# The opening of a one-core transformer layer: x in four whole-tile loads, whole-tile squares, half tiles scaled on GpSimd, and a shorter refinement

## The chip, the core and the metric

The kernel runs on one core of one Trainium2 chip. The metric is the device time of one execution in microseconds (us). The kernel before has a median of 902.12 us in 3 runs (900.91 to 902.39). One execution of it was also profiled; its time is 901.98 us, of which the profile's span, from the first instruction to the last, holds 900.2 us.

Five engines work side by side and meet at semaphores: TensorE (PE for the matmuls, PEld for the weight loads that overlap them), VectorE (DVE), ScalarE (ACT), GpSimd (POOL) and SyncE (SP), which here issues nearly all the loads. Each engine runs its own instructions strictly in order.

## The reference

The reference is one layer of a diffusion backbone in fp32: 512 latent tokens x of width 1024, 256 context tokens, and a conditioning vector c. Cut to what the change touches:

```
shift, scale, ... = split(silu(c) @ w_ada + b_ada, 6)
hx = (x * rsqrt(mean(x*x) + 1e-6) * norm1_g) * (1 + scale) + shift
z  = hx @ w_in            # u, vs, q, r, ga, gb, k, v, lr
... gated linear attention, spatial gating, merge, residual
... second norm, gated convolution FFN, residual, final norm
```

The same modulation, with another vector `c_ctx`, is made for the context tokens. So before the first product with `w_in` the kernel needs two things: x normalised and turned (features on the partitions), and the first 128 columns of the shift and the scale, which need the first columns of `w_ada`.

## The kernel before

**Tiling.** Tokens come in four tiles of 128 rows, features in eight blocks of 128 columns. Every large product is made from three fp32r matmuls: each operand is split into a high part and a low part, and high by high, high by low and low by high are added up in PSUM. The matmuls of these products fill nearly all of the span.

**The opening.** `tok_load` (line 142) brings x in as eight loads of 128 by 512 fp32 (256 KB) on SP's queue, two for each token tile. Four short rows (c, c_ctx, norm1_g, b_ada) come in on ACT's queue into one tile of 72 rows, which PE turns once (line 489). While x arrives, PE runs seven matmuls on constants (line 598), whose results are thrown away. `norm_tiles` (line 542) goes over the tiles: ACT squares each half (line 519, with its sum), DVE adds the two sums and makes mean plus epsilon (lines 523 and 524), ACT makes `exp(-0.5 ln v)` as a first estimate of the reciprocal root (lines 525 and 526), DVE refines it with one Newton step in three instructions (lines 531 to 533), and DVE scales both halves (lines 536 and 540); of the last tile ACT scales the second half (line 538).

`x_turns` (line 572) then turns six of the eight feature blocks of a tile on PE (line 565), each into its own PSUM bank. For tile 0 it also makes `silu(c)` on DVE and ACT (lines 497 to 501). Tiles 2 and 3 are turned together, after the first modulation sum.

**Modulation.** The columns of shift and scale are made in six groups (four of 128 columns, two of 256). `ada_load` (line 327) loads a group's part of `w_ada`; `ada_dot` (line 625, matmuls at line 634) sums it over the features with `silu(c)` as the weights, a copy takes the sums out of PSUM (line 582 for group 0), `ada_sel` (line 638) turns them into columns with two tiny matmuls (line 643) and makes the factor `am` and the addend `bm_` on DVE (lines 647 and 653). `ada_mod` (line 655) then writes a block's high part on ACT (line 664), its exact value and its low part on DVE (lines 665 and 671), and after it come the first products (line 725): q and k of head 0 and v of heads 0 and 1, block by block, while the next group's `w_ada` arrives. After the first block ACT copies turned blocks 2, 4 and 5 out of PSUM (line 570); block 1 is copied just before it.

**What sets the order.** SP's loads go out in the order of the program: x, group 0 of `w_ada`, the first rows of q, k and v weights, group 1, the next rows, and so on (lines 372 to 389); `in_order` ties them. From `STRICT` (line 561) to line 842 the instructions of PE, ACT and DVE are tied to the order of the program as well; GpSimd and SP are not named in that tie. SP's and ACT's loads share eight semaphores in rotation, and a load that takes a semaphore waits until the earlier load on it has landed.

**Buffers.** x lies in eight of the 43 `heap` tiles, and so do the squares' unused outputs. The stream of split weights uses the pool `wp`, with five buffers each for `raw`, `wh` and `wl`; four of each belong to the first v weights `fv` from the start.

Of the kernel before, what the change touches and what calls it, by code (L numbers as in the profile page):

```python
# [16 lines left out]
P = 128  # L17
# [30 lines left out]
def backbone_kernel(  # L48
# [20 lines left out]
    def nm(s):  # L69
        cnt[0] += 1  # L70
        return f"{s}_{cnt[0]}"
# [4 lines left out]
    def late(shape, dt=F32, s="l"):  # L76
        return lp.tile(shape, dt, tag="l", name=nm(s))

    def small(n, s="s"):
        return sp.tile([P, n], F32, tag=f"sm{n}", name=nm(s))  # L80

    def mm():
        return pm.tile([P, 512], F32, tag="mm", name=nm("mm"))

    def gl():
        return pg.tile([P, 512], F32, tag="gl", name=nm("gl"))
# [48 lines left out]
    adma = nc.scalar.dma_start  # L135
    A.preload_act_table_set("natural_log_exp_and_others")

    rows_a = late([72, P], s="rows")
    for o, ap in ((0, c[0]), (8, c_ctx), (16, norm1_g[0]), (24, b_ada[0])):
        adma(rows_a[o:o + ap.shape[0] // P, :], r8(ap))  # L140

    def tok_load(ap, n, pool):
        tiles = []
        for t in range(n):
            pair = [pool([P, 512], s="xin") for _ in range(2)]
            for hf in range(2):
                dma(pair[hf], ap[t * P:(t + 1) * P, hf * 512:(hf + 1) * 512])
            tiles.append(pair)
        return tiles

    START = len(traced())
    xin = tok_load(x[0], 4, heap)

    specs = []

# [329 lines left out]
        V.tensor_copy(cols_, ps[:, :n])  # L485
        return cols_

    rows_ps = mm()
    T.transpose(rows_ps[:, :72], rows_a, ident[:72, :72])
    vec_a = const([P, 72], "vec_a")  # L490
    cT, n1g, bada = vec_a[:, 0:16], vec_a[:, 16:24], vec_a[:, 24:72]
    cs = const([P, KT, 32], "cs")
    V.memset(cs, 0.0)

    def silu_c():
        sg = small(16, "sg")
        A.activation(sg, cT, AF.Exp, scale=-1.0)
        V.tensor_scalar(sg, sg, 1.0, None, op0=ALU.add)
        V.reciprocal(sg, sg)
        V.tensor_tensor(cs[:, :, 0], cT[:, 0:8], sg[:, 0:8], op=ALU.mult)  # L500
        V.tensor_tensor(cs[:, :, 1], cT[:, 8:16], sg[:, 8:16], op=ALU.mult)

    selm = const([P, 4], "selm")
    for i in range(4):
# [27 lines left out]
        V.scalar_tensor_tensor(t_, t_, -0.5, v, op0=ALU.mult, op1=ALU.mult)  # L532
        V.scalar_tensor_tensor(r, t_, 1.5, r, op0=ALU.add, op1=ALU.mult)

    def norm_scale(pair, r, split=False):
        V.tensor_scalar(pair[0], pair[0], r, None, op0=ALU.mult)
        if split:
            A.mul(pair[1], pair[1], r)
        else:
            V.tensor_scalar(pair[1], pair[1], r, None, op0=ALU.mult)  # L540

    def norm_tiles(tiles, then):

        n = len(tiles)
        ss = [small(2, "ss") for _ in range(n)]
        todo = [(t, hf) for t in range(n) for hf in range(2)]
        sq = lambda: norm_sq(tiles[todo[0][0]], todo[0][1], ss[todo.pop(0)[0]]) if todo else None
        vr = [None] * n
        sq()
        for t in range(n + 1):  # L550
            if t:
                rstd_b(*vr[t - 1])
            if t < n:
                sq()
                sq()
                vr[t] = rstd_a(ss[t])
            if t:
                norm_scale(tiles[t - 1], vr[t - 1][1], t == n)
                then(t - 1)

    STRICT = len(traced())
    xps = [(mm, gl)[k > 3]() for k in range(6)]

    def x_turn(ps, t, k):
        T.transpose(ps[:, t * P:(t + 1) * P], xin[t][k // 4][:, (k % 4) * P:(k % 4 + 1) * P], ident)

    fx = [None] + [heap([P, S], s="xT") for _ in range(KT - 1)]

    def x_out(k, ps, eng):
        eng(fx[k], ps)  # L570

    def x_turns(t):
        if t == 0:
            V.tensor_copy(vec_a, rows_ps[:, :72])
            V.tensor_scalar(bsc1, bada[:, 8:16], 1.0, None, op0=ALU.add)
            silu_c()
        if t < 2:
            for k in range(6):
                x_turn(xps[k], t, k)
        elif t == 3:  # L580
            dot0.extend(ada_dot(0))
            V.tensor_copy(*dot0)
            for k in range(6):
                for tt in (2, 3):
                    x_turn(xps[k], tt, k)
                if k == 1:
                    ada_sel(0, dot0[0])
            one_hi(fqk[0], 0)
            x_out(1, xps[1], A.copy)

    def x_late(k):
        ps = gl()
# [1 line left out]
            x_turn(ps, t, k)  # L594
        x_out(k, ps, A.copy)

    for i in range(7):
        T.matmul(xps[1][:, :256], ones, ident.unsqueeze(1).to_broadcast([P, 2, P]), start=True, stop=True)

    am, bm_ = const([P, KT, 2], "am"), const([P, KT, 2], "bm")  # L600

# [8 lines left out]
    def one_hi(z, kk):  # L610
        raw, wh, _ = ((q[:, :, kk] if z in fqk else q[:, kk]) for q in z)
        A.copy(wh, raw)
# [9 lines left out]

    hx, hc, fc = [], [], []

    def ada_dot(g):

        cg = GROUPS[g] * P
        wa = was.pop(g)
        nk = 512 // cg
        aps = gl()  # L630
        for k in range(KT):
            for kind in range(2):
                j = kind + 2 * (k % 2)
                T.matmul(aps[32 * j:32 * j + 32, :cg], cs[:, k, :], wa[2 * (k // nk) + kind][:, k % nk, :],
                         start=(k < 2), stop=(k >= KT - 2), tile_position=(0, 32 * j))
        return [heap([P, cg], s="asb"), aps[:, :cg]]
# [126 lines left out]
            V.tensor_tensor(st[32:64, :], raw[32:64, :], st[32:64, :].bitcast(F32), op=ALU.subtract)  # L763
            w2s.append(st)

    dot0 = []
    norm_tiles(xin, x_turns)
    one_lo(fqk[0], 0)
    ada_mod(0)
    one_hi(fv[0], 0)  # L770
    one_lo(fv[0], 0)
    x_out(2, xps[2], A.copy)
    x_out(4, xps[4], A.copy)
    x_out(5, xps[5], A.copy)
# [1215 lines left out]
```

## Time and profile before

| what | value |
|---|---|
| median of 3 runs | 902.12 us (900.91 to 902.39) |
| the profiled execution, and its span | 901.98 us, 900.2 us |
| PE busy | 886.5 us (98% of the span) |
| PEld busy | 739.9 us (82%) |
| DVE, ACT, POOL busy | 743.4, 482.2, 85.3 us |
| mean rate of the transfers | 218 GB/s |

The profile lists groups of instructions with their source line, the engine, the tile written and the tiles read. "Idle before" is time in which an engine had nothing running just before a group, with what ended it. A weight load that overlaps a matmul is counted under PEld. Matmuls are pipelined and their ends are modelled, so starts are the better guide. The DMA share is the busy share of the core's 16 DMA engines taken together; overlapping packets can bring it above 1. All stretches of time below are counted from the start of the span.

### The profile page before, as it was taken

Reading aid. Unit: us, or ns where it says so; the run is one execution under the profiler, and the core shown is the slowest. Engines: PE = TensorE matmul, PEld = TensorE weight load, DVE = VectorE, ACT = ScalarE, POOL = GpSimd, SP = SyncE. Lnnn points to the kernel's source line nnn. Section 1 sums busy time; section 2 is a strip of 40 time slices with the busy share of each in tenths; the row PEclk is TensorE's granted clock in tenths of the full one; section 3 lists DMA queues with packets and bytes.
Section 4 is the critical chain, followed back from the end, with each engine's and each line's share of the span. In section 5 each row is a group of like instructions: output and inputs, shape, how many; then the busy total and the mean of one; then the engine's idle time right before and its main releaser. Section 6 shows DMA issues by size and latency. Waiting matters only on the chain.

```text
span 900.2 us, 12525 instructions
## 1 busy us (share of the span) xinstructions
PE 886.5 (98%) x4461; PEld 739.9 (82%) x4461; DVE 743.4 (83%) x1235; ACT 482.2 (54%) x801; POOL 85.3 (9%) x134
## 2 busy tenths in 40 slices
PE   6999999999999999999999999999999999999997
PEld 5778888988888888888888889888888888888886
DVE  6468777969889899689998658887899987897997
ACT  6256454857676665767433348433443334365763
POOL 1312223221000000000000010001111110000000
PEclk9999999999999999999999999999999999999999
DMA  9985999999268678777994951898999893247462
GB/s 280 355 270 123 292 281 216 231 332 211 71 214 263 195 252 263 239 234 253 383 339 148 307 166 57 282 307 172 195 215 177 178 195 97 88 149 228 153 195 109
DMA packets 155308, 196.12 MB, mean 218 GB/s; under 512 B 9273, under 2 KB 88453, under 8 KB 155245
## 3 DMA queue, kind: packets, MB, share of 16 engines
q1 hardware_dynamic: 131229, 137.39, 48.3%
q0 software_dynamic: 21024, 52.65, 26.4%
q10 hardware_dynamic: 2992, 5.28, 1.6%
q8 instruction: 35, 0.57, 0.3%
q14 instruction: 28, 0.23, 0.1%
HBM read 186.90 MB, written 58.72 MB: 273 GB/s over the span
## 4 chain that ended last, share of the span: by engine, by line
PE 93%; SPq 2%; DMA 2%; DVE 1%; ACT 1%; issue 0%; DVEq 0%; ACTq 0%
PE mm L425 34%; PE mm L1384 15%; PE mm L443 11%; PE gl L1866 10%; PE gl L1384 6%; PE gl L961 3%; PE mm L1866 2%; PE mm L725 1%; DMA wa<-in_w_ada_dram 1%; PE mm L1073 1%; PE mm L1123 1%; PE gl L443 1%; SPq L335 1%; PE gl L996 1%; PE gl L1253 1%; SPq L356 1%
## 5 line engine op out<-in xcount | busy, mean ns | idle before, releaser
L279 ACT CAST wh<-raw 128x1024 fp32r<-128x1024 f32 x189 | 195.0, 1037 | 176.4 <-PE mm L425 90.1
L280 DVE TENSOR_TENSOR wl<-raw,wh 128x1024 fp32r<-128x1024 f32 x189 | 225.7, 1200 | 45.6 <-ACT wh L279 44.5
L425 PE MATMUL mm<-h2h,wh 128*128 128x512 f32 (+1 forms) x344 | 133.0, 387 | 0.0
L425 PE MATMUL mm<-h2l,wh 128*128 128x512 f32 (+1 forms) x344 | 133.0, 387 | 0.0
L425 PE MATMUL mm<-h2h,wl 128*128 128x512 f32 (+1 forms) x344 | 133.0, 387 | 0.0
L1717 DVE SCALAR_TENSOR_TENSOR cacc<-ca,ccol,cacc 128x441 f32<-128x441 f32 (+2 forms) x176 | 121.9, 695 | 4.4
L425 PEld LDWEIGHTS mm<-h2h,wl 128*128 128x128 f32 x344 | 64.6, 188 | 13.2
L425 PEld LDWEIGHTS mm<-h2l,wh 128*128 128x128 f32 x344 | 64.6, 188 | 13.2
L425 PEld LDWEIGHTS mm<-h2h,wh 128*128 128x128 f32 x344 | 64.6, 188 | 13.0
L1866 PE MATMUL gl<-wl,dah 128*128 128x512 f32 (+1 forms) x132 | 50.6, 383 | 0.0
L1866 PE MATMUL gl<-wh,dal 128*128 128x512 f32 (+1 forms) x132 | 50.6, 383 | 0.0
L1866 PE MATMUL gl<-wh,dah 128*128 128x512 f32 (+1 forms) x132 | 50.6, 383 | 0.0
L238 POOL DMA_DIRECT2D sum<-in_ffn_w_down_dram x24 | 13.2, 554 | 377.2 <-PE mm L443 258.3
L1214 DVE SCALAR_TENSOR_TENSOR acc<-wa,cs,acc 128x512 f32<-128x512 f32 x64 | 46.4, 746 | 0.0
L1718 ACT ACTIVATE cacc<-cacc 128x512 f32<-128x512 f32 x22 | 13.9, 632 | 59.2 <-DVE cacc L1717 59.2
L1384 PE MATMUL mm<-wh,xs 128*128 128x512 f32 x128 | 41.1, 392 | 0.0
L425 PE MATMUL mm<-hxh,wh 128*128 128x512 f32 x104 | 40.9, 393 | 0.0
L425 PE MATMUL mm<-hxl,wh 128*128 128x512 f32 x104 | 40.6, 391 | 0.0
L425 PE MATMUL mm<-hxh,wl 128*128 128x512 f32 x104 | 40.5, 390 | 0.0
L1384 PE MATMUL mm<-wh,hxh 128*128 128x512 f32 x96 | 37.7, 393 | 0.0
L1384 PE MATMUL mm<-wh,hxl 128*128 128x512 f32 x96 | 37.4, 390 | 0.0
L1384 PE MATMUL mm<-wl,hxh 128*128 128x512 f32 x96 | 37.4, 390 | 0.0
(483 smaller groups left out, 2017.2 us busy)
## 6 DMA issues: line engine op xcount, KB each, us to landing
raw<-in_w_in_dram SPq DMA_DIRECT2D x52, 512.0 KB
wa<-in_w_ada_dram SPq DMA_DIRECT2D x96, 256.0 KB
raw<-sum SPq DMA_DIRECT2D x46, 512.0 KB
raw<-in_ffn_w_up_dram SPq DMA_DIRECT2D x44, 512.0 KB
sum<-in_ffn_w_down_dram POOLq DMA_DIRECT2D x30, 512.0 KB, 6.4
sum<-in_w_in_dram POOLq DMA_DIRECT2D x28, 512.0 KB, 8.2
sum<-sum POOLq DMA_DIRECT2D x22, 512.0 KB, 6.3
raw<-in_ffn_w_down_dram SPq DMA_DIRECT2D x15, 512.0 KB
```

Of the source, the lines that this page charges most:

```text
L238: behind_pe(lambda: G.dma_start(sums[b][dst], ap), G)
L279: A.copy(wh, raw)
L280: V.tensor_tensor(wl, raw, wh.bitcast(F32), op=ALU.subtract)
L335: dma(t_, w_ada[0, kp * nk * P:(kp + 1) * nk * P, c0:c0 + cg].rearrange("(k p) c -> p k c", p=P))
L425: T.matmul(ps, a[:, k, :], b[:, c0:c0 + n], start=(k == 0 and i == 0), stop=(k == KT - 1 and i == 2))
L443: T.matmul(ps, a[:, t * P:(t + 1) * P], b[:, k % 2, :], start=(k == 0 and i == 0), stop=(k == KT - 1 and i == 2))
L961: T.matmul(ps, p_, q_, start=(start and z == 0), stop=(stop and z == 2))
L1214: behind_last(lambda: V.scalar_tensor_tensor(acc[i], coming.pop(0), cs[:, k, 0:1], acc[i], op0=ALU.mult, op1=ALU.add), V)
L1384: T.matmul(banks[t], a(kk, t), w[:, kk, :], start=(first and b == 0 and kk == 0 and i == 0), stop=(b == 1 and kk == 1 and i == 2), skip_gr ...
L1717: V.scalar_tensor_tensor(o, a_[:, r0 + dy:r1 + dy, c0 + dx:c1 + dx], wcol(tap), o, op0=ALU.mult, op1=ALU.add)
L1718: A.activation(acc, acc, AF.Gelu)
L1866: T.matmul(ps, a, w[:, kk, cols], start=(first and kk == 0 and i == 0), stop=(last and kk == n_ - 1 and i == 2), skip_group_check=True)
```

## The change

- x comes in as four loads of 128 by 1024 (512 KB), one for each token tile, into the buffers of `wl` and `wh` in turn, in place of eight loads into heap tiles.
- ACT squares a whole tile of 1024 columns in one instruction; the unused output lies in a `raw` buffer. The addition of two half sums falls away.
- The four short rows come into two tiles: c and c_ctx (16 rows), turned first, and norm1_g and b_ada (56 rows), turned later.
- The refinement is written as two instructions: `t = r*v*r`, then `r = (t - 3)*r`; the missing factor of -0.5 is applied with the scaling (for the last tile by an instruction of its own).
- DVE scales the first half of tiles 0 to 2, GpSimd the second half; for tile 3, DVE and ACT as before.
- Of the silu, GpSimd does the addition and the two products, DVE the reciprocal.
- The warm-up matmuls are three of 256 columns that read x's tile 1, and later two and one of 128 columns on constants, in place of seven on constants.
- The tiles are turned one by one, tile 2 after group 0's modulation sum and tile 3 after `ada_sel`. That sum goes into the PSUM bank that the rows and warm-ups use, and is copied out by ACT in place of DVE.
- The copy of block 1 moves from before the first modulation to after it, ahead of the copies of blocks 2, 4 and 5.

```diff
-    rows_a = late([72, P], s="rows")
-    for o, ap in ((0, c[0]), (8, c_ctx), (16, norm1_g[0]), (24, b_ada[0])):
-        adma(rows_a[o:o + ap.shape[0] // P, :], r8(ap))
+    rows_c, rows_n = late([16, P], s="rows"), late([56, P], s="rows")
+    for rows, o, ap in ((rows_c, 0, c[0]), (rows_c, 8, c_ctx), (rows_n, 0, norm1_g[0]), (rows_n, 8, b_ada[0])):
+        adma(rows[o:o + ap.shape[0] // P, :], r8(ap))
...
-    xin = tok_load(x[0], 4, heap)
+    xin = []
+    for t in range(4):
+        z = wp.tile([P, 2, 512], F32, tag=("wl", "wh")[t % 2], name=nm("xin"))
+        dma(z, x[0][t * P:(t + 1) * P, :].rearrange("p (h c) -> p h c", h=2))
+        xin.append(z)
...
     def silu_c():
-        sg = small(16, "sg")
-        A.activation(sg, cT, AF.Exp, scale=-1.0)
-        V.tensor_scalar(sg, sg, 1.0, None, op0=ALU.add)
+        G.tensor_scalar(sg, sg, 1.0, None, op0=ALU.add)
         V.reciprocal(sg, sg)
-        V.tensor_tensor(cs[:, :, 0], cT[:, 0:8], sg[:, 0:8], op=ALU.mult)
-        V.tensor_tensor(cs[:, :, 1], cT[:, 8:16], sg[:, 8:16], op=ALU.mult)
+        G.tensor_tensor(cs[:, :, 0], cT[:, 0:8], sg[:, 0:8], op=ALU.mult)
+        G.tensor_tensor(cs[:, :, 1], cT[:, 8:16], sg[:, 8:16], op=ALU.mult)
...
+    def x_square(t):
+        junk = wp.tile([P, 2, 512], F32, tag="raw", name=nm("junk"), bufs=RAW).bitcast(BF16)[:, 0, :].rearrange(
+            "p (h c) -> p h c", h=2)
+        ss = small(1, "ss1")
+        A.activation(junk, xin[t], AF.Square, accum_out=ss)
+        return ss
+    def x_factor(ss):
+        v, r, t_ = small(1, "v"), small(1, "r"), small(1, "t")
+        V.tensor_scalar(v, ss, 1.0 / D, EPS, op0=ALU.mult, op1=ALU.add)
+        A.activation(r, v, AF.Ln)
+        A.activation(r, r, AF.Exp, scale=-0.5)
+        return v, r, t_
+    def x_refine(v, r, t_):
+        V.scalar_tensor_tensor(t_, r, v, r, op0=ALU.mult, op1=ALU.mult)
+        V.scalar_tensor_tensor(r, t_, -3.0, r, op0=ALU.add, op1=ALU.mult)
+        return r
+    def x_half(t, hf, eng, r):
+        z = xin[t][:, hf, :]
+        if eng is A:
+            A.mul(z, z, r)
+        else:
+            eng.tensor_scalar(z, z, r, -0.5, op0=ALU.mult, op1=ALU.mult)
+    def x_open():
+        for i in range(3):
+            T.matmul(turn_ps[:, :256], ones, xin[1][:, i // 2, i % 2 * 256:i % 2 * 256 + 256], start=True, stop=True)
+        T.transpose(turn_ps[:, 256:272], rows_c, ident[:16, :16])
+        ss = [x_square(0), x_square(1)]
+        def turns(t):
+            for k in range(6):
+                x_turn(xps[k], t, k)
+        f = x_factor(ss[0])
+        r = x_refine(*f)
+        x_half(0, 0, V, r)
+        x_half(0, 1, G, r)
+        turns(0)
+        ss.append(x_square(2))
+        f1 = x_factor(ss[1])
+        V.tensor_copy(vec_a[:, :16], turn_ps[:, 256:272])
+        A.activation(sg, cT, AF.Exp, scale=-1.0)
+        f2 = x_factor(ss[2])
+        silu_c()
+        ss.append(x_square(3))
+        r = x_refine(*f1)
+        x_half(1, 0, V, r)
+        x_half(1, 1, G, r)
+        warm(WARM[0])
+        T.transpose(turn_ps[:, 272:328], rows_n, ident[:56, :56])
+        warm(WARM[1])
+        turns(1)
+        V.tensor_copy(vec_a[:, 16:], turn_ps[:, 272:328])
+        V.tensor_scalar(bsc1, bada[:, 8:16], 1.0, None, op0=ALU.add)
+        dot = ada_dot(0, turn_ps)
+        r = x_refine(*f2)
+        f3 = x_factor(ss[3])
+        x_half(2, 0, V, r)
+        x_half(2, 1, G, r)
+        turns(2)
+        A.copy(*dot)
+        r = x_refine(*f3)
+        V.tensor_scalar(r, r, -0.5, None, op0=ALU.mult)
+        x_half(3, 1, A, r)
+        V.tensor_scalar(xin[3][:, 0, :], xin[3][:, 0, :], r, None, op0=ALU.mult)
+        ada_sel(0, dot[0])
+        turns(3)
+        one_hi(fqk[0], 0)
+    def warm(n):
+        for _ in range(n):
+            T.matmul(turn_ps[:, :P], ones, ident, start=True, stop=True)
...
-    for i in range(7):
-        T.matmul(xps[1][:, :256], ones, ident.unsqueeze(1).to_broadcast([P, 2, P]), start=True, stop=True)
...
-    def ada_dot(g):
+    def ada_dot(g, bank=None):
...
-        aps = gl()
+        aps = bank if bank is not None else gl()
...
-    dot0 = []
-    norm_tiles(xin, x_turns)
+    x_open()
     one_lo(fqk[0], 0)
     ada_mod(0)
     one_hi(fv[0], 0)
     one_lo(fv[0], 0)
+    x_out(1, xps[1], A.copy)
     x_out(2, xps[2], A.copy)
```

More of the change, by code (lines that the diff above doesn't have):

```diff
@@ L486, in columns @@
         return cols_
-    rows_ps = mm()
-    T.transpose(rows_ps[:, :72], rows_a, ident[:72, :72])
     vec_a = const([P, 72], "vec_a")
@@ L493, in backbone_kernel @@
     V.memset(cs, 0.0)
+    sg = small(16, "sg")
     def silu_c():
-        sg = small(16, "sg")
-        A.activation(sg, cT, AF.Exp, scale=-1.0)
-        V.tensor_scalar(sg, sg, 1.0, None, op0=ALU.add)
+        G.tensor_scalar(sg, sg, 1.0, None, op0=ALU.add)
         V.reciprocal(sg, sg)
-        V.tensor_tensor(cs[:, :, 0], cT[:, 0:8], sg[:, 0:8], op=ALU.mult)
-        V.tensor_tensor(cs[:, :, 1], cT[:, 8:16], sg[:, 8:16], op=ALU.mult)
+        G.tensor_tensor(cs[:, :, 0], cT[:, 0:8], sg[:, 0:8], op=ALU.mult)
+        G.tensor_tensor(cs[:, :, 1], cT[:, 8:16], sg[:, 8:16], op=ALU.mult)
     selm = const([P, 4], "selm")
@@ L533, in rstd_b, with norm_scale @@
         V.scalar_tensor_tensor(r, t_, 1.5, r, op0=ALU.add, op1=ALU.mult)
[L535 to L540, printed above, removed]
+    def norm_scale(pair, r):
+        for z in pair:
+            V.tensor_scalar(z, z, r, None, op0=ALU.mult)
     def norm_tiles(tiles, then):
@@ L557, in norm_tiles @@
             if t:
-                norm_scale(tiles[t - 1], vr[t - 1][1], t == n)
+                norm_scale(tiles[t - 1], vr[t - 1][1])
                 then(t - 1)
@@ L562, in backbone_kernel @@
     xps = [(mm, gl)[k > 3]() for k in range(6)]
+    turn_ps = gl()
+    WARM = (2, 1)
     def x_turn(ps, t, k):
-        T.transpose(ps[:, t * P:(t + 1) * P], xin[t][k // 4][:, (k % 4) * P:(k % 4 + 1) * P], ident)
+        T.transpose(ps[:, t * P:(t + 1) * P], xin[t][:, k // 4, (k % 4) * P:(k % 4 + 1) * P], ident)
     fx = [None] + [heap([P, S], s="xT") for _ in range(KT - 1)]
@@ L570, in x_out @@
         eng(fx[k], ps)
[L572 to L577, printed above, removed]
+    def x_square(t):
[4 more added lines that the diff above has]
+        return ss
@@ L578, in x_turns @@
+    def x_open():
[4 more added lines that the diff above has]
+        def turns(t):
             for k in range(6):
                 x_turn(xps[k], t, k)
[L580 to L589, printed above, removed]
+        f = x_factor(ss[0])
[33 more added lines that the diff above has]
+        one_hi(fqk[0], 0)
```

## The prediction

> **What bounds the kernel now.** I read the stretches first (busy time of each engine in windows), then the chain of waits, then the timeline of the opening and SP's own waits.
>
> ```profile
> 6.00:16.67 10.67, 9.83 (x73) 7.71 (x74) 7.38 (x37) 7.94 (x26) 0.00 (x0) 1.00 1.01 305
> 16.67:35.50 18.83, 18.83 (x166) 14.45 (x166) 11.03 (x25) 7.61 (x14) 5.87 (x11) 1.00 1.07 337
> 35.50:38.20 2.70, 2.63 (x34) 1.20 (x34) 0.02 (x1) 0.00 (x0) 2.00 (x4) 1.00 1.09 363
> 38.20:60.00 21.80, 21.59 (x122) 16.60 (x123) 14.32 (x34) 9.75 (x22) 3.17 (x6) 1.00 1.09 360
> 150.00:300.00 150.00, 150.00 (x788) 128.59 (x787) 129.68 (x238) 99.60 (x185) 15.95 (x21) 1.00 0.81 217
> ```
>
> Columns are the stretch, its length, busy PE, PEld, DVE, ACT and POOL, the granted clock, the DMA share and GB/s. From 16.67 us on PE hardly stops, so an opening that lets PE's products start earlier is worth what it gains there, if nothing later holds PE at a fixed time. Up to 60 us something may: the DMA share stands at 1.07 to 1.09, and the loads come in a fixed order. The chain of waits shows that hold:
>
> ```profile
> 30.46 6.98 DMA wa<-in_w_ada_dram
> 37.45 0.04 issue
> 37.49 0.63 PE gl L634 x6
> ```
>
> ```profile
> 35.51 2.61 PE L634 MATMUL gl<-wa,cs 128*32 128x256 f32 x32
> ```
>
> ```profile
> 46.98 1.93 PE L634 MATMUL gl<-wa,cs 128*32 128x256 f32 x32
> ```
>
> The last piece of `w_ada`'s group 4, issued at 30.46, lands at 37.45 us, and PE's sum over it, which takes 1.93 us when nothing is late (group 5), took 2.61: 0.68 us of waiting. PE is on the heels of the loads here. The same holds at the start, where the opening's path runs:
>
> ```profile
> 3.72 0.63 ACT L519 ACTIVATE junk<-xin 128x512 bf16<-128x512 f32 x1 [1.64 <-DMA xin<-in_x_dram]
> 4.96 0.63 ACT L519 ACTIVATE junk<-xin 128x512 bf16<-128x512 f32 x1 [0.51 <-DMA xin<-in_x_dram]
> ...
> 11.20 0.61 ACT L519 ACTIVATE junk<-xin 128x512 bf16<-128x512 f32 x1
> ...
> 13.99 0.64 PE L634 MATMUL gl<-wa,cs 128*32 128x128 f32 x14 [0.41 <-DMA wa<-in_w_ada_dram]
> ...
> 14.56 0.66 PE L565 MATMUL mm<-ident,xin 128*128 128x128 f32 x4
> 14.69 0.29 DVE L582 COPY asb<-gl 128x128 f32<-128x128 f32 x1 [0.62 <-PE gl L634]
> ...
> 15.05 0.37 PE L643 MATMUL gl<-selm,asb 128*128 128x4 f32 x2
> ...
> 15.46 0.28 DVE L647 TENSOR_SCALAR am<-gl,bsc,vec_a 128x2 f32<-128x2 f32 x1 [0.48 <-PE gl L643]
> ...
> 15.84 0.78 ACT L664 ACTIVATE hxh<-mm,bm,am 128x512 fp32r<-128x512 f32 x1
> ```
>
> Group 0 of `w_ada` is late (PE waits until 13.99); sum, copy, selection, `am` and the first high part at 15.84 follow it without slack. x is normalised only just in time for its place between them.
>
> **The loads.** The supply in this stretch and SP's own waits:
>
> ```profile
> 2.00:3.50 1.50, 0.00 (x0) 0.00 (x0) 1.20 (x7) 0.08 (x1) 1.04 (x5) 1.00 0.87 270
> 3.50:5.00 1.50, 0.00 (x0) 0.00 (x0) 0.00 (x0) 0.76 (x3) 0.00 (x0) 1.00 0.83 251
> 5.00:7.00 2.00, 1.01 (x3) 0.94 (x4) 0.31 (x2) 1.67 (x7) 0.00 (x0) 1.00 0.91 333
> 7.00:9.00 2.00, 2.00 (x6) 1.56 (x5) 1.73 (x9) 1.56 (x8) 0.00 (x0) 1.00 0.85 226
> 9.00:11.00 2.00, 2.00 (x9) 1.62 (x9) 1.75 (x11) 1.58 (x6) 0.00 (x0) 1.00 1.07 343
> ```
>
> ```profile
> SPq L147 <- DMA xin<-in_x_dram: 2.1, 3, 1.0
> ```
>
> ```profile
> 0.81 5.50 SPq L147 DMA_DIRECT2D xin<-in_x_dram  x8
> ```
>
> SP needs 5.50 us to issue the eight loads of x, 2.1 of them waiting for earlier pieces of x to land, because twelve early loads share eight semaphores. The DMA engines run below their later level (share 0.83 to 0.91, against 1.07 with 343 GB/s). With four loads of x and four rows all eight go out without a wait, and only the first `w_ada` pieces wait, with up to 2 MB queued ahead of them. From 2 to 9 us the rows give 0.41 + 0.38 + 0.67 + 0.45 = 1.90 MB; at 343 GB/s it would be 2.40. The missing 0.50 MB is **1.46 us** of transfer, and everything behind x in the queue moves up by as much: group 0 from 13.99 to 12.5 us, group 4 from 37.45 to 36.0. Bounds: 0.7 us if only half the deficit is a matter of waiting and the rest is starting up; 2.2 us if x runs at the rate of 5 to 7 us brought to full share (333 x 1.07 / 0.91 = 392 GB/s). I take 1.5, since three windows out of four fall short by a like amount. The number of bytes is the same.
>
> **The opening's own work.** Tile 0 is whole where the second half was squared, 4.9 us; the others follow at 343 GB/s, 0.524 MB in 1.5 us each: 6.4, 8.0, 9.5. Durations:
>
> ```profile
> L279 ACT CAST wh<-raw 128x1024 fp32r<-128x1024 f32 x189 | 195.0, 1037 | 176.4 <-PE mm L425 90.1
> ```
>
> ```profile
> L519 ACT ACTIVATION_READ_ACCUMULATOR junk<-xin 128x1 f32 x8 | 1.5, 187 | 0.0
> ...
> L526 ACT ACTIVATE r<-r 128x1 f32<-128x1 f32 x4 | 0.8, 203 | 0.1
> ...
> L536 DVE TENSOR_SCALAR xin<-xin,r 128x512 f32<-128x512 f32 x4 | 1.9, 479 | 0.0
> ...
> L533 DVE SCALAR_TENSOR_TENSOR r<-t,r 128x1 f32<-128x1 f32 x4 | 0.6, 160 | 0.1
> ...
> L325 POOL MEMSET w2r<- 96x512 f32 x2 | 1.0, 514 | 0.0
> ...
> L125 POOL TENSOR_SCALAR_AFFINE_SELECT maskb<-ones 128x128 f32<-128x128 f32 x1 | 0.3, 283 | 0.0
> ```
>
> A whole-tile square is priced as ACT's 1024-column cast, 1.04 us, plus 0.19 for the sum. ACT in order: squares of tiles 0 and 1 end at 7.6, two small ones for tile 0's factor 8.0, square of tile 2 9.2, five small ones (tile 1's factor, the silu's exponential, tile 2's factor, 0.2 each) 10.2, square of tile 3 11.4. The refinement is 0.16 us shorter and the sum of halves (0.16) is gone, yet these lie beside ACT's queue and I count them at nothing. Tile 1 is refined after the reciprocal at 10.5, scaled on DVE by 11.3 and on GpSimd by 11.7, and turned by 12.0; then comes the sum over group 0, whose last tiles land at 12.5: it ends at 13.05 (half of its 32 matmuls after the landing). ACT's copy takes 0.3, six turns of tile 2 stand ahead of the selection on PE (0.8), selection 0.4, `am` and `bm_` 0.35: the first high part starts at **14.65 us, not 15.84, 1.2 us earlier**. Tile 3 (factor at 12.6, halves scaled by 14.2) and its turns fit beside that.
>
> GpSimd's half tile is in no row. Its own rows bound it: 0.51 us for a fill of 512 columns, 1.13 for four times the 128-column select. I take 0.8, between them, as scaling reads and writes like the select but pays the start once. Three of its halves lie on the path, one behind the other only through the sums, so the bounds move the first high part by about 0.3 us each way. GpSimd has no other work from its fills until `fx` is written, so nothing is queued behind the halves:
>
> ```profile
> 17.78 0.75 POOL L847 DMA_DIRECT2D fx<-xT  x1 [14.74 <-DVE xT L665]
> ```
>
> [...]
>
> **After the first high part.** Block 1's copy now stands ahead of those of blocks 4 and 5:
>
> ```profile
> 17.50 1.08 ACT L570 COPY xT<-gl 128x512 f32<-128x512 f32 x2
> ...
> 18.79 0.81 PEld L634 LDWEIGHTS gl<-wa,cs 128*32 128x32 f32 x32 [0.38 <-ACT xT L570]
> ```
>
> The next sum takes a bank that these copies free. They ended 2.74 us after the first high part began, and PE took the bank 2.95 after; with one more copy of 0.59 ahead they end 3.33 after. That costs 0 (if block 4's bank is the one) to 0.4; I take 0.2. So PE is 1.0 us ahead at group 1. At group 4 it also no longer needs to wait its 0.68 us if the load is early enough: PE alone could then be 1.7 us ahead, the load allows 1.5. **The smaller holds: 1.5 us.** After 38 us PE loses only 0.21 us up to 60 and nothing from 150 to 300, so the lead is kept; a load is no longer late there, as group 5's sum ran at full pace.
>
> Other edits cost nothing: the rows' second turn and the one and two warm-ups beside it stand on a PE that then waits for tile 1; were that cover gone, they would cost some 0.5 us. x in `wl` and `wh` buffers delays only the fourth v weights' split, in a block that comes after x's last turn.
>
> Sum, against the profiled execution: 901.98 - 1.5 = **900.5 us**. It lies 0.14 under the median shown, so against that the gain is 1.6.
>
> **The rivals.**
>
> *The stream doesn't move.* The 16 DMA engines may be slow at the start for a reason of their own: 251 GB/s came from 3.5 to 5 us though up to four loads were outstanding. Then group 4 still lands within 0.3 us of 37.45 and PE, early, waits there: 901.98 - 0.3 = 901.7. Against it: SP's waits of 2.1 us are real, and the share falls to 0.85 again at 7 to 9.
>
> *GpSimd sets the pace.* If a half tile takes its upper 1.13 us and waits 0.48 for DVE's half each time, tiles 1 and 2 come 0.8 us later each, one of them ahead of the sum: it ends at 13.85 to 14.0, the high part starts at 15.6, and with the copies PE gains nothing until group 4, where its 0.68 us of waiting go: 901.98 - 0.6 = 901.4.
>
> *The clock stays low: slower.* PE's warm-ups show a clock that needs time:
>
> ```profile
> 5.99 0.35 PE L489 MATMUL mm<-ident,rows 72*128 72x72 f32 x1 [5.99 <-DMA rows<-in_b_ada_dram]
> ```
>
> ```profile
> 7.07:9.63 2.56, 2.56 (x7) 2.02 (x6) 1.00 0.85 249
> 9.63:10.95 1.32, 1.32 (x7) 0.99 (x5) 1.00 1.12 347
> ```
>
> In the two stretches (line 598 alone; PE, PEld) a matmul of one kind starts about every 0.43 us, then every 0.22, some 3.6 us after PE's first work (5.99); the granted clock reads 1.00 in both. The new warm-ups wait for tile 1 (6.4 us), run 3 x 2 x 0.43 = 2.6 us at the low rate, and then PE has turns with gaps. If the doubling comes only in the first products, turns and sum before them cost 1.7 us more (about 1.7 us of PE work on the path at half rate), the first products 1.8 us (3.6 us at half rate): 3.5 lost, 1.0 + 0.68 regained: 901.98 + 1.8 = 903.8. It decides if PE is too little busy between 9 and 13 us. Against it: before, the gap ahead of 13.99 (0.41 us) cost no clock.
>
> [...]
>
> **How the numbers follow.** The forecast 0.58 (its own range 899.7 to 901.2, from 0.7 and 2.2 us of transfer); the unmoved stream 0.18; GpSimd's pace 0.12; the low clock 0.12. About 0.2% (1.8 us) is what a measurement of this kernel can tell from no change. The forecast lies just inside: of its 0.58 some 0.30 fall beyond 1.8 us, as its upper bounds and the median's 0.14 help it; 0.05 more from a shift of later waits. Faster 0.35, slower 0.10 (most of the low clock's case), same 0.55. Range 899.3 to 902.9: below the forecast's own by run-to-run spread (the three runs span 1.5), above through the two middle rivals, short of the low clock.
>
> **What would show it.** Right: SP's wait on x gone; share above 1 by 6 us; group 0's last sum near 12.5; first high part near 14.7; group 4's wait near 36 or none. Wrong: group 4 still at 37.4 (first rival), GpSimd halves above 1.2 us (second), matmuls at line 725 every 0.43 us (third), or a new wait after 60 us.

## The result, and the profile after

The changed kernel has a median of 900.2 us in 21 runs (899.61 to 902.32), against 902.12 us in 21 runs of the kernel before (900.91 to 903.74): a ratio of 0.9982 (95% interval 0.9976 to 0.9989), a gain of 1.9 us. By the ratio that is 0.18%, just inside the 0.2% (1.8 us) that the prediction called no telling difference, and by the medians just outside it; the interval leaves no doubt of its sign. The forecast was 900.5 us.

Eighteen of the 21 times lie at 899.61 to 900.84, three at 902.19 to 902.32, and the execution that was profiled is one of the three (902.19 us, span 900.5 us), so the views below show the changed kernel with something gone wrong; the first experiment profiles it again.

The stretches of the changed kernel (stretch, its length, busy PE, PEld, DVE, ACT, POOL, granted clock, DMA share, GB/s):

```profile
2.00:3.50 1.50, 0.00 (x0) 0.00 (x0) 1.20 (x7) 0.08 (x1) 1.04 (x5) 1.00 0.85 284
3.50:5.00 1.50, 0.00 (x0) 0.00 (x0) 0.00 (x0) 0.57 (x1) 0.00 (x0) 1.00 1.03 397
5.00:7.00 2.00, 1.17 (x3) 1.02 (x4) 0.15 (x1) 1.79 (x5) 0.00 (x0) 1.00 1.00 378
7.00:9.00 2.00, 2.00 (x7) 1.13 (x6) 0.94 (x5) 1.68 (x6) 0.89 (x1) 1.00 1.04 352
...
16.67:35.50 18.83, 18.22 (x165) 13.85 (x164) 11.51 (x27) 8.73 (x16) 5.48 (x10) 1.00 1.04 333
35.50:38.20 2.70, 2.70 (x34) 1.69 (x36) 0.00 (x0) 0.00 (x0) 1.71 (x4) 1.00 1.12 372
```

The supply changed as the prediction's first step says: from 3.5 to 9 us the DMA engines are full (1.00 to 1.04, before 0.83 to 0.91), and 397, 378 and 352 GB/s stand where 251, 333 and 226 stood. SP's own waits in the first 12 us show where the waiting went:

```profile
SPq L339 <- DMA xin<-in_x_dram: 2.1, 2, 1.7
```

SP waits as long as before, but at the first pieces of `w_ada` (line 339), with all of x already queued. In the trace's transfers the last piece of `w_ada`'s group 0 lands at 11.69 us (13.95 before) and of group 4 at 34.67 (37.45 before). The second limit, PE's wait at group 4, is gone: in the last stretch above PE is busy for all of 35.5 to 38.2 us, and PE's timeline has the sum without a stall (start, duration, engine, line, operation, tiles, shape, count, and idle time before with what ended it):

```profile
5.83 2.90 PE L603 MATMUL gl<-xin,ones 128*128 128x256 f32 x6 [5.83 <-DMA xin<-in_x_dram]
8.66 0.28 PE L604 MATMUL gl<-ident,rows 16*128 16x16 f32 x1
8.88 1.11 PE L566 MATMUL mm<-ident,xin 128*128 128x128 f32 x4
...
13.49 1.91 PE L692 MATMUL gl<-wa,cs 128*32 128x128 f32 x32
15.33 0.66 PE L566 MATMUL mm<-ident,xin 128*128 128x128 f32 x4
...
17.64 0.73 PE L783 MATMUL gl<-hxh,qkh 128*128 128x512 f32 x2 [0.60 <-ACT hxh L722]
...
36.73 1.93 PE L692 MATMUL gl<-wa,cs 128*32 128x256 f32 x32
```

What went wrong is in the same rows. Four turns take 1.11 us at 8.88 and 0.66 at 15.33; the sum over group 0, 32 matmuls, takes 1.91 us, where the runs below show 1.08. PE worked without a pause from 5.83 us and still ran at about half rate until some 15 us, with the granted clock reading 1.00 throughout. ACT's timeline gives the consequence, and the price of a whole-tile square:

```profile
4.43 1.06 ACT L577 ACTIVATE junk<-xin 128x1024 bf16<-128x1024 f32 x1 [2.35 <-DMA xin<-in_x_dram]
5.39 0.19 ACT L577 ACTIVATION_READ_ACCUMULATOR junk<-xin 128x1 f32 x1
...
16.81 0.78 ACT L722 ACTIVATE hxh<-mm,bm,am 128x512 fp32r<-128x512 f32 x1
```

The first high part is at 16.81 us, 0.97 later than before. All the same this execution's span is only 0.25 us longer than before's, because PE no longer waits 0.68 us at group 4.

### The profile page after: what moved, and what is told of

The parts are those of the page before. It is cut to its first block, busy times and chain, and to the rows that moved or that the text cites. A ratio compares the mean times of both kernels' runs of the same rounds, so it can differ in the third digit from the quotient of the medians.

```text
span 900.5 us, 12521 instructions
## 1 busy us (share of the span) xinstructions
PE 887.4 (99%) x4460; PEld 740.9 (82%) x4460; DVE 741.4 (82%) x1223; ACT 481.0 (53%) x793; POOL 88.9 (10%) x140
## 4 chain that ended last, share of the span: by engine, by line
PE 93%; DMA 3%; SPq 2%; DVE 1%; ACT 1%; issue 0%; DVEq 0%; ACTq 0%
PE mm L429 34%; PE mm L1442 15%; PE mm L447 11%; PE gl L1924 10%; PE gl L1442 6%; PE gl L1019 3%; PE mm L1924 2%; DMA wa<-in_w_ada_dram 2%; PE mm L1131 1%; PE mm L1181 1%; PE mm L783 1%; PE gl L447 1%; SPq L360 1%; PE gl L1054 1%; DMA qkraw<-in_w_in_dram 1%; PE gl L1311 1%
## 5 line engine op out<-in xcount | busy, mean ns | idle before, releaser
L429 PEld LDWEIGHTS mm<-h2h,wh 128*128 128x128 f32 x344 | 64.6, 188 | 13.1
L429 PEld LDWEIGHTS mm<-h2h,wl 128*128 128x128 f32 x344 | 64.6, 188 | 13.1
L1776 ACT ACTIVATE cacc<-cacc 128x512 f32<-128x512 f32 x22 | 13.9, 632 | 59.1 <-DVE cacc L1775 59.1
```

What stands on the lines that cost most here:

```text
L429: T.matmul(ps, a[:, k, :], b[:, c0:c0 + n], start=(k == 0 and i == 0), stop=(k == KT - 1 and i == 2))
L1776: A.activation(acc, acc, AF.Gelu)
```

## The experiments

The theory after this profile: two limits race in the first 60 us, PE's own start (the first high part, and with it the clock) and the landing of group 4; the later one decides, and after that PE's lead or lag is kept to the end. "Clock" here and below is the rate at which matmuls follow each other; the granted clock of the profile reads 1.00 in every stretch shown. Rivals: the four loads alone make the gain (or have no part in it), GpSimd's halves cost something, and the late landings come from the writes of `fx` that share the transfer engines. The table has each profiled execution by its anchors, read from the instructions and transfers of its trace; times are us from the start of the span, "first" is the first high part, "sum 4" the first and last matmul's start in the sum over group 4, "last" the start of the last of the first products.

| kernel | first | sum 4 | group 0 landed | group 4 landed | last | span |
|---|---|---|---|---|---|---|
| before | 15.84 | 35.51–37.74 | 13.95 | 37.45 | 61.44 | 900.24 |
| after | 16.81 | 36.73–38.28 | 11.69 | 34.67 | 61.95 | 900.49 |
| after_again | 15.26 | 35.15–36.71 | 13.10 | 36.27 | 60.44 | 898.97 |
| early_warm | 14.13 | 34.00–37.38 | 11.94 | 37.08 | 61.07 | 899.56 |
| early_warm_2 | 14.02 | 33.91–35.46 | 11.53 | 34.36 | 59.16 | 897.64 |
| before_four_loads | 16.07 | 35.75–37.31 | 12.41 | 34.30 | 61.03 | 899.55 |
| after_eight_loads | 15.92 | 35.82–37.82 | 13.83 | 37.52 | 61.75 | 900.52 |
| no_warm | 16.46 | 36.34–37.89 | 12.06 | 34.54 | 61.59 | 900.09 |
| dve_halves | 14.59 | 34.46–36.51 | 12.16 | 36.21 | 60.20 | 898.71 |
| copy_first | 15.57 | 35.23–37.26 | 12.27 | 36.97 | 60.98 | 899.50 |
| late_fx | 15.24 | 35.11–36.67 | 12.10 | 32.94 | 60.36 | 898.83 |
| early_warm_late_fx | 14.45 | 34.32–35.88 | 12.24 | 34.14 | 59.57 | 898.10 |
| early_warm_late_fx_2 | 14.51 | 34.39–35.95 | 12.25 | 33.80 | 59.66 | 898.15 |
| before_late_fx | 15.51 | 35.17–36.73 | 13.62 | 35.08 | 60.43 | 900.48 |

Two readings carry the rest. The span less "last" is 838.5 to 838.8 us in all rows but the bottom one, so whatever the change does is done by 61 us. And a sum over group 4 that isn't held up takes 1.55 us from first to last start; where it takes longer, its end follows the landing by 0.3 us (before, early_warm, after_eight_loads, copy_first, dve_halves).

**The changed kernel again.** No edit.

> The changed kernel unaltered, for a profile of another execution. Clock theory: the profiled execution at 902.19 us kept the low clock until about 15 us because its warm-ups and turns left gaps, and the executions near 900.1 reach the full clock earlier; so an execution near 900.1 shows the sum over group 0 in about 1.1 us (not 1.9) and the first high part near 14.7 us (not 16.8). Rival (later chance): executions near 900.1 have the same opening to within 0.3 us and differ after 60 us. Time by either: 900.2 us, most runs 899.6 to 900.8.

Measured: 900.18 us (899.64 to 900.89, 11 runs) against 901.99 for the kernel before beside it, ratio 0.9978 (0.9969 to 0.9987). PE's timeline of this execution, 900.70 us:

```profile
5.78 2.90 PE L603 MATMUL gl<-xin,ones 128*128 128x256 f32 x6 [5.78 <-DMA xin<-in_x_dram]
8.61 0.28 PE L604 MATMUL gl<-ident,rows 16*128 16x16 f32 x1
8.82 1.11 PE L566 MATMUL mm<-ident,xin 128*128 128x128 f32 x4
...
11.43 0.52 PE L649 MATMUL gl<-ident,ones 128*128 128x128 f32 x2
11.85 0.66 PE L566 MATMUL mm<-ident,xin 128*128 128x128 f32 x4
...
12.78 1.08 PE L692 MATMUL gl<-wa,cs 128*32 128x128 f32 x32
```

Up to 11.4 us PE does the same work at the same times, within 0.05 us, as in the execution of 902.19 us. Then the rate doubles here, and there it doubles at about 15 us. The sum takes 1.08 in place of 1.91 us, the first high part is at 15.26 in place of 16.81 (14.7 was expected), and the 1.55 us of earlier start come out as 1.52 us of span. So the kernel is the same and the time at which its clock rises is not. That the other two times of 902.2 and 902.3 us have this cause wasn't profiled. This execution, 900.70 us, is one of the slower ordinary ones: it shows 1.3 of the 1.9 us that the medians are apart, and no profile shows the unaltered kernel at its median of 900.2. Nor are its loads as steady as those above: from 5 to 7 us the DMA share falls to 0.82 (288 GB/s), and group 0 lands at 13.10.

The step from 11.5 to about 15 us is some 3.5 us long. Three more profiles below begin with the same PE work (late_fx, copy_first, dve_halves) and double at 11.6, 10.7 and 10.0 us, so over the five the spread is 5 us. What sets the moment no run shows.

**Warm-ups that don't wait for x.** Five matmuls on constants go ahead of the three that read x:

```diff
+        for i in range(5):
+            T.matmul(turn_ps[:, :256], ones, ident.unsqueeze(1).to_broadcast([P, 2, P]), start=True, stop=True)
         for i in range(3):
             T.matmul(turn_ps[:, :256], ones, xin[1][:, i // 2, ...], start=True, stop=True)
```

> The changed kernel with five more warm-ups of 256 columns on constants ahead of the three that read x, so PE works from about 1.6 us. Clock theory: full clock before 9 us in every execution, first high part near 14.3 us, no runs near 902.2, median 899.7 to 900.1 and a spread under 1 us. Rival (the clock does not matter, or turns never bring it up): the same median as the changed kernel, 900.2, with runs near 902.2 still among them.

Measured: 900.16 us (899.27 to 902.23, 11 runs), ratio 0.998 (0.997 to 0.999). The spread was expected under 1 us, with no time near 902.2, and is 3 us with one at 902.23. PE's timeline:

```profile
5.89 1.56 PE L605 MATMUL gl<-xin,ones 128*128 128x256 f32 x6
...
11.64 1.08 PE L694 MATMUL gl<-wa,cs 128*32 128x128 f32 x32
...
34.00 1.75 PE L694 MATMUL gl<-wa,cs 128*32 128x256 f32 x24
35.91 0.62 PE L694 MATMUL gl<-wa,cs 128*32 128x256 f32 x2 [0.16 <-DMA wa<-in_w_ada_dram]
37.12 0.63 PE L694 MATMUL gl<-wa,cs 128*32 128x256 f32 x6 [0.60 <-DMA wa<-in_w_ada_dram]
```

The six matmuls of the three warm-ups on x take 1.56 us where they took 2.90: the clock is up by 6 us. The first high part starts at 14.13 us, the time at which the prediction had it less 0.5. None of that reached the end in this execution: `w_ada`'s last piece of group 4 lands at 37.08, PE waits for it, and the lead of 1.7 us over before shrinks to 0.4. So an early clock doesn't rule out a late execution. The same kernel was measured a second time, on another chip.

> The same as early_warm, for a second profile and more times, beside the next kernel on one chip. Load theory: again the first high part is near 14.3 us and PE waits for group 4 (its sum longer than 1.6 us from first to last start), 900.0 to 900.3. Rival (the piece that landed at 37.08 was a chance): no wait there, and a span of 898.0 (14.3 + 883.7): 899.5 to 899.7.

Measured: 899.37 us (899.15 to 901.23, 10 runs) against 901.9, ratio 0.9975 (0.9965 to 0.9984). The two medians of this one program are 0.8 us apart, which says how little a difference of half a microsecond between two experiments proves here. PE was expected to wait for group 4 again; it landed at 34.36, and PE's timeline has no wait:

```profile
33.91 1.93 PE L694 MATMUL gl<-wa,cs 128*32 128x256 f32 x32
```

Same program, same start (14.02 and 14.13), and 1.9 us between the two spans, nearly all of it from when one piece landed. The trace has sixteen landings for the piece. In the late case they lie between 33.14 and 37.08 us; fifteen are there by 34.69, and the last alone comes 2.4 us later. In early_warm_2 the last is 0.9 us behind the fifteenth. Why one of them falls behind in some executions stays open.

**The loads alone.** The kernel before, with x in four loads and nothing else changed:

```diff
-    xin = tok_load(x[0], 4, heap)
+    xin = []
+    for t in range(4):
+        z = wp.tile([P, 2, 512], F32, tag=("wl", "wh")[t % 2], name=nm("xin"))
+        dma(z, x[0][t * P:(t + 1) * P, :].rearrange("p (h c) -> p h c", h=2))
+        xin.append([z[:, 0, :], z[:, 1, :]])
```

> The kernel before with nothing but x in four whole-tile loads into the wl and wh buffers. Stream theory: group 0 of w_ada lands near 11.7 us (not 13.95), group 4 near 34.7 to 35.5 (not 37.45), PE no longer waits there, and the gain is 0.7 us (the wait at group 4) to 1.5 us: 900.6 to 901.4. Rival (the gain needs the new order of the opening): the loads land earlier but the first high part stays at 15.8 us or later, and the time is 901.9 to 902.1.

Measured: 901.49 us (901.03 to 902.81, 11 runs), ratio 0.9994 (0.9985 to 1.0002): 0.5 us better, which can't be told from nothing and is less than the 0.7 to 1.5 expected. The loads did move (group 0 to 12.41, group 4 to 34.30), and the wait at group 4 is gone. But the opening doesn't use it. The chain of waits up to 9 us and PE's timeline:

```profile
2.12 5.31 DMA rows<-in_b_ada_dram
```

```profile
9.51 3.02 PE L602 MATMUL mm<-ident,ones 128*128 128x256 f32 x10
```

The single turn of all four rows, and behind it the seven warm-ups, wait for the last row, `b_ada`. It takes 5.31 us, with the four loads of 512 KB issued ahead of it or beside it, and PE starts at 7.57 us (5.99 before). The warm-ups then stand in front of x, and the first high part is at 16.07. PE lost 0.23 us at the start and got 0.68 back at group 4: some 0.4 us, which the "last" column shows (61.44 to 61.03).

**The rest without the loads.** The changed kernel, with eight loads again:

```diff
-        dma(z, x[0][t * P:(t + 1) * P, :].rearrange("p (h c) -> p h c", h=2))
+        for h in range(2):
+            dma(z[:, h, :], x[0][t * P:(t + 1) * P, h * 512:(h + 1) * 512])
```

> The changed kernel with x in eight half-tile loads again, into the same buffers. Stream theory: group 0 lands near 14 us and group 4 near 37.4 again, so at least 1.3 us of the gain of 1.9 goes: 901.5 to 902.1. Rival (opening's own order): squares and scaling in the new order keep most of the gain: 900.2 to 900.9.

Measured: 902.05 us (901.38 to 903.19, 11 runs), ratio 1.0 (0.9992 to 1.0009). The whole gain is gone. SP's waits and PE's timeline:

```profile
SPq L156 <- DMA xin<-in_x_dram: 2.4, 3, 1.0
```

```profile
13.03 1.48 PE L693 MATMUL gl<-wa,cs 128*32 128x128 f32 x32
...
35.82 2.38 PE L693 MATMUL gl<-wa,cs 128*32 128x256 f32 x32
```

SP waits between the loads of x again, group 0 lands at 13.83 and stretches its sum from 1.08 to 1.48 us, and group 4 lands at 37.52 and holds PE as it held it before. The loads alone are worth 0.5 us, the rest alone nothing (0.06 us the wrong way), both together 1.8. The loads alone move the landings (34.30) and not PE's start (16.07). The rest alone moves neither: tile 1 of x and group 0 land later again (its warm-ups start at 6.39 us, group 0 is there at 13.83), and the first high part is at 15.92, though its clock is up by 10.2 us. Here the new opening is worth something only with the earlier loads.

**No warm-ups.** The changed kernel without the three warm-ups on x and the three on constants (which compute nothing that is used):

```diff
-        for i in range(3):
+        for i in range(0):
...
-    WARM = (2, 1)
+    WARM = (0, 0)
```

> The changed kernel without any of its six warm-ups (three on x, two and one on constants). Clock theory: PE then has only turns, in short runs, until the sum over group 0; the low clock lasts into the first products, the first high part comes at 15.3 to 16.8 us and up to 1.8 us more are lost in the products: 901.8 to 903.5. Rival (warm-ups are of no use, the turns bring the clock up): 900.2 and the first high part near 15.2.

Measured: 900.8 us (900.27 to 902.17, 11 runs), ratio 0.9988 (0.9977 to 0.9999). PE's timeline:

```profile
8.32 1.11 PE L566 MATMUL mm<-ident,xin 128*128 128x128 f32 x4 [2.50 <-DVE v L583]
...
12.35 1.94 PE L692 MATMUL gl<-wa,cs 128*32 128x128 f32 x32
14.21 1.12 PE L566 MATMUL mm<-ident,xin 128*128 128x128 f32 x4
15.12 0.64 PE L566 MATMUL gl<-ident,xin 128*128 128x128 f32 x2
...
15.84 0.74 PE L566 MATMUL mm<-ident,xin 128*128 128x128 f32 x4
```

Turns and sum all run at the low rate; the clock rises at about 16 us, within the four turns at 15.84 and before the first products. So the products are not slow, and the 901.8 to 903.5 us expected didn't come. The first high part is at 16.46, and in this execution the kernel loses 1.1 us of span against after_again; by the medians it loses 0.6. So a clock that comes late goes with a loss of about a microsecond here, and 1.5 us between the two profiles of the changed kernel; nothing behind the first high part runs slowly in any of them. Between these two kernels the clock isn't the only difference, as the warm-ups take PE's time as well: after, whose clock comes some 0.8 us sooner, has its first high part at 16.81.

**DVE scales both halves.** GpSimd is taken out of tiles 0 to 2:

```diff
-        x_half(0, 1, G, r)
+        x_half(0, 1, V, r)
...
-        x_half(1, 1, G, r)
+        x_half(1, 1, V, r)
...
-        x_half(2, 1, G, r)
+        x_half(2, 1, V, r)
```

> The changed kernel with the second halves of tiles 0 to 2 scaled on DVE in place of GpSimd. GpSimd's half measured 0.85 to 0.98 us beside DVE's 0.48, so the two halves in a row on DVE (0.96) end at about the same time; but DVE's next work starts 0.48 later, three times. GpSimd as a gain: first high part 0.3 to 0.5 us later, 900.4 to 900.7. Rival (GpSimd sets the pace, as the second rival of the prediction has it): the first high part comes 0.3 us or more earlier, 899.7 to 900.0.

Measured: 900.12 us (899.71 to 901.04, 11 runs) against 902.14, ratio 0.9978 (0.9969 to 0.9987), the same as the changed kernel's. GpSimd's rows in the changed kernel, and DVE's and PE's in this one:

```profile
7.89 0.89 POOL L599 TENSOR_SCALAR xin<-xin,r 128x512 f32<-128x512 f32 x1 [4.85 <-DVE r L591]
...
10.53 0.85 POOL L599 TENSOR_SCALAR xin<-xin,r 128x512 f32<-128x512 f32 x1
13.15 0.98 POOL L599 TENSOR_SCALAR xin<-xin,r 128x512 f32<-128x512 f32 x1 [1.77 <-DVE v L583]
```

```profile
12.24 0.88 DVE L599 TENSOR_SCALAR xin<-xin,r 128x512 f32<-128x512 f32 x2
13.03 0.21 DVE L590 SCALAR_TENSOR_TENSOR t<-r,v 128x1 f32<-128x1 f32 x1
```

```profile
9.89 0.47 PE L566 MATMUL gl<-ident,xin 128*128 128x128 f32 x2
```

GpSimd takes 0.85 to 0.98 us for a half tile while DVE does the other; DVE does both, one behind the other, in 0.88. Handing half of the scaling to GpSimd shows no gain and no loss at the median. The profile is less even: its first high part is at 14.59 us, 0.67 before after_again's, as the rival had it. But its clock is up at 10.0 us (two turns take 0.47; 0.64 at the low rate), 1.5 us before after_again's, so how much of that is GpSimd's stays open. PE then waits some 0.5 us for group 4, which lands at 36.21.

**Block 1's copy at its old place.**

```diff
         one_hi(fqk[0], 0)
+        x_out(1, xps[1], A.copy)
...
     one_hi(fv[0], 0)
     one_lo(fv[0], 0)
-    x_out(1, xps[1], A.copy)
```

(The copy stands at the end of `x_open` here, as it ended the last step of `x_turns` before.)

> The changed kernel with ACT's copy of block 1 back ahead of the first modulation. Prediction's step (the moved copy holds the next bank by 0 to 0.4 us): from the first high part to group 1's sum 2.95 us again, not 3.17, and the high part itself starts later by up to 0.59 if ACT is the last to be ready. Sum: 900.0 to 900.7. Rival (no difference): 3.17 us again and 900.2.

Measured: 900.52 us (899.83 to 901.2, 11 runs), ratio 0.9981 (0.9972 to 0.999). ACT's timeline:

```profile
14.70 0.39 ACT L671 CAST qkh<-qkraw 128x256 fp32r<-128x256 f32 x1
15.09 0.59 ACT L571 COPY xT<-mm 128x512 f32<-128x512 f32 x1
15.57 0.78 ACT L723 ACTIVATE hxh<-mm,bm,am 128x512 fp32r<-128x512 f32 x1
```

From the first high part to group 1's sum it takes 2.94 us, against 3.17 with the copy moved (15.26 to 18.43 in after_again): the move costs 0.2 there. But at its old place the copy puts 0.48 us between the cast and the first high part, on ACT, which has no slack in the new opening. By these two rows the move is a gain of some 0.25 us; the medians (900.52 and 900.12 to 900.18 for the other two) lean the same way without proving it.

**The writes of `fx` later.** The eight turned blocks of x are written out on GpSimd's queue from 17 to 19 us on (256 KB each), among the loads. In this experiment the writes wait for PE's last instruction behind the first products (the low-rank sum, near 63 us):

```diff
+    fs_end = next(z for z in reversed(traced()) if z.engine == T.engine)
     k1 = splits.pop(0)
...
+        start = len(traced())
         G.dma_start(d, fx[k])
+        for i in traced()[start:]:
+            if i.engine == G.engine:
+                tc.add_manual_dep(i, fs_end.name, ...)
```

> The changed kernel with the eight writes of fx held back until near 62 us, warm-ups as they are. Load theory: group 4's last piece lands by 35 us in the profile, PE never waits for it, and the time follows the first high part alone (span end 883.7 us after it): 899.6 to 900.0, with the spread that the clock gives. Rival (the early warm-ups alone made the 899.27): 900.2 and group 4 after 36 us.

Measured on the changed kernel: 899.87 us (899.71 to 900.57, 11 runs) against 901.9, ratio 0.9981 (0.9972 to 0.9989). Group 4 lands at 32.94, the earliest of all, and the times lie within 0.9 us of each other. The median isn't told apart from the changed kernel's; there PE's own start already set the end.

> The kernel before with nothing but the eight writes of fx held back. Load theory: group 4 lands 1.5 to 2.2 us earlier than 37.45, PE's wait of 0.68 us there goes, the first high part stays near 15.8: 901.3 to 901.6. Rival (the writes are harmless): 902.1.

Measured on the kernel before: 902.19 us (901.95 to 902.69, 11 runs), ratio 1.0003 (0.9995 to 1.0012): no gain, though the wait at group 4 is gone (landing 35.08) and PE is 1.0 us ahead at 60 us. This is the one row of the table that gives its lead back, and the trace shows where. DVE's timeline of the kernel before, then GpSimd's, DVE's and PE's of this one:

```profile
67.51 0.43 DVE L695 CAST hch<-hcf 128x512 fp32r<-128x512 f32 x1 [0.59 <-ACT hcf L691]
```

```profile
63.00 4.34 POOL L849 DMA_DIRECT2D fx<-xT  x8 [26.68 <-PE gl L706]
67.33 1.00 POOL L863 MEMSET pmask<- 128x512 f32 x2
```

```profile
66.50 2.12 DVE L695 CAST hch<-hcf 128x512 fp32r<-128x512 f32 x1 [0.61 <-ACT hcf L691]
```

```profile
67.06 0.60 PE L682 MATMUL gl<-ident,xin 128*128 128x128 f32 x4
68.67 0.50 PE L1129 MATMUL mm<-wh,hch 128*128 128x512 f32 x1 [1.02 <-DVE hch L695]
```

The eight writes, all issued at once, occupy GpSimd from 63.0 to 67.3 us and two fills follow it to 68.3. A cast of the context's first block on DVE takes 2.12 us beside them, 0.43 without, and ends 0.3 us after GpSimd's fills; PE waits 1.02 us for it. From one row to the next on PE it is 1.61 us, 0.36 in the kernel before: the missing 1.25. In late_fx the same cast meets the same work, but the losses are 0.4 us each at two casts (66.43 and 67.88), and PE doesn't wait for either:

```profile
66.43 0.81 DVE L753 CAST hch<-hcf 128x512 fp32r<-128x512 f32 x1 [0.91 <-ACT hcf L749]
...
67.88 0.77 DVE L753 CAST hch<-hcf 128x512 fp32r<-128x512 f32 x1
```

What lengthens the casts beside GpSimd's work no run shows.

**Both together.** The five early warm-ups and the late writes on the changed kernel, measured twice:

> The changed kernel with the five early warm-ups and, besides, the eight writes of fx (256 KB each, GpSimd's queue) held back until the first products and the low-rank sums of PE are done, near 62 us. Load theory: with a first high part at 14.1 us the kernel is held by group 4's last piece (37.08 us with the early warm-ups alone, so that they gained nothing); three writes of 256 KB, about 0.7 us of transfer each, lie ahead of that piece, so it lands by 35 us, PE's sum over group 4 ends near 35.6 and the span ends near 897.8: 899.0 to 899.6. Rival (the piece is late for another reason, such as one slow engine): group 4 still lands after 36.5 us and the time stays at 900.0 to 900.3.

Measured: 899.27 us (899.12 to 900.07, 6 runs) against 902.14, ratio 0.9971 (0.9959 to 0.9982).

> The same as early_warm_late_fx, for more times. Load theory: 899.1 to 899.5 median, 0.6 us or more under early_warm of the same call. Rival (both are held by the same thing): within 0.3 us of early_warm.

Measured: 899.29 us (899.21 to 899.87, 6 runs) against 901.9, ratio 0.9971 (0.996 to 0.9983). In both profiles group 4 lands by 34.2, before PE's last matmuls of the sum need it, and the first high part starts at 14.5. This version beats both kernels: its twelve times lie at 899.12 to 900.07, eight of them under the lowest of the changed kernel's 32 (899.61). Against early_warm_2, measured beside it (899.37), the late writes gain 0.1 us at the median, not the 0.6 expected; early_warm's times run up to 902.23 the first time and 901.23 the second, so what they seem to remove is the late executions. With 12 and 21 times that isn't proved.

## Why the prediction was right, step by step

**The time: right.** 900.5 was forecast and 900.2 measured, in the forecast's own range; the gain of 1.6 against the median is 1.9.

**The loads move up 1.5 us: right, and a little low.** With four loads of x the last piece of group 0 lands at 11.5 to 13.1 us (eleven executions, most near 12.2), with eight at 13.6 to 14.0 (three). So the 1.5 us lies within the prediction's bounds, and some 1.7 is typical. For group 4 a single figure was the wrong form: it was put at 36.0, and the executions with four loads, and the writes left where they were, have it between 34.3 and 37.1. The sum read the landing of 37.45 in one profile as a fixed time.

**The opening's own work, 1.2 us earlier: the mis-sized term.** The first high part was forecast at 14.65; it came at 15.26, 0.6 us earlier than before, and in the slower execution at 16.81, later than before. The step that failed is the one that turned tile 1 "by 12.0" and ended the sum at 13.05: it priced PE's turns and sum at the full rate. In after_again PE works from 5.78 us to the end of the sum with no gap over 0.2 us, at half rate up to 11.4; the sum ends at 13.9, not 13.05. early_warm is the check of that: with the clock up before the first turns (the sum takes 1.08 us in all four profiles with early warm-ups) the first high part is at 14.0 to 14.5, where the rest of the working had it.

**GpSimd's half tile at 0.8 us: a little low, without effect.** It takes 0.85 to 0.98, inside the bounds, and taking GpSimd out leaves the median where it was.

**The moved copy, 0.2 us: right where it was priced, but half the account.** Behind the first high part it costs 0.2. What it frees ahead of it on ACT, 0.48 us, was not in the sum; together, by rows of two profiles, it is a gain of some 0.25.

**"The smaller holds": the wrong one of the two.** The sum let PE be 1.7 us ahead at group 4 and the load allow 1.5. In both profiles of the changed kernel the load was early (34.67, 36.27) and PE set the end: in after_again 0.4 us at group 1, 0.68 more from the wait that is gone, 1.0 at the last of the first products, and 1.27 in the span. The forecast's 1.5 us was approached, in that profile, with less from the opening and nothing lost to the load, and the medians are apart by 0.6 us more than these rows account for. So a part of its closeness is luck.

**The lead is kept after 38 us: right.** From the last first product to the end it is 838.5 to 838.8 us in thirteen of fourteen profiles.

**The rivals.** The stream that doesn't move fell (group 0's landing, share above 1 from 3.5 us). GpSimd's pace fell by its price (0.85 to 0.98 us, not 1.13 and 0.48 of waiting) and by the median of dve_halves. That a half tile on GpSimd waits 0.48 us for DVE's half was supposed, and no run shows it: in after GpSimd's three halves start 0.06 to 0.19 us behind DVE's, before these end. The low clock is real: in the profiled execution of the changed kernel the clock comes after the sum, as that rival said. But its price was put too high, 903.8: the 1.8 us for slow first products never came, because the clock was up before them in every profile, no_warm's included. One profiled execution shows it, and there it takes the gain; three of 32 times of the unedited kernel stand near 902.2, and early_warm, profiled at 901.27 with its clock up early, shows that a late load alone can cost as much (1.9 us against early_warm_2). What raises the clock no run settles. In before the rate doubled some 3.6 us after PE's first work (9.63 against 5.99 us); PE worked with no gap over 0.2 us for 5.6 us in after_again and for more than 9 us in after until it doubled. The doubling came behind the sum in after and no_warm, and before the sum in after_again and all the other profiles; all but no_warm have warm-ups ahead of their turns. no_warm comes nearest to turns alone: PE ran nothing else from 8.32 to 12.35 us, with one pause of 0.73 us, and stayed at the low rate; the rate doubled some 3.6 us after the sum began. Counted from PE's first matmul that is not a turn, the doubling comes after 3 to 6 us in thirteen of the fourteen profiles and after 9.3 in after. Whether no_warm's turns count for nothing or its pause held the doubling back, these profiles can't tell.

## What to carry to other kernels

When two limits lie close together (here PE's start and the landing of a load), an edit that moves one may show nothing by itself: test the halves apart and together before either is thrown away. In the ten profiles without early warm-ups PE's matmuls ran at half rate until 9.6 to 16 us, so price such a start at half rate unless the profile shows matmuls of one kind at the full rate. Let warm-ups begin on constants, not on data that arrive late: with five of them the full rate was there by 8.5 us, and the first high part at 14.0 to 14.5 in place of 14.6 to 16.8. A piece of work pushed to another time, like GpSimd's writes here, must be checked against what runs there, since the same edit kept its lead on one kernel and lost all of it on the other.

## What the runs showed of the hardware that was not expected

- One kernel with the same PE work at the same times within 0.05 us up to 11.4 us got the full matmul rate at 11.5 us in one execution and about 15 us in another, and the granted clock read 1.00 all along. That is 1.5 us of the span, nearly as much as the whole change gains.
- The last piece of one group of loads landed at 34.4 us in one execution and 37.1 in another of the same program, where the last of its sixteen parts came 2.4 us behind the other fifteen.
- A DVE cast of 128 by 512 took 2.12 us beside GpSimd's DMA issues and fills, 0.43 without. On a small scale it is there in the changed kernel too. DVE's timeline in after_again, where GpSimd scales its half from 12.82 to 13.80:

```profile
13.30 0.52 DVE L590 SCALAR_TENSOR_TENSOR t<-r,v 128x1 f32<-128x1 f32 x1
```

  The same one-column instruction takes 0.21 us in dve_halves, and here it ends when GpSimd's half does.
- A row of 24 KB (`b_ada`) that was issued at 2.12 us landed 5.31 us later, with four loads of 512 KB issued ahead of it or beside it (before_four_loads).
